# Branch B's scan with the two directions' chunks in one 128x128 product, the backward direction running the sample first

## The chip, the cores and the metric

The kernel runs on one core of one Trainium2 chip. The metric is the device time of one execution in microseconds (us). A core has a matrix engine (TensorE, PE), three others that compute (VectorE DVE, ScalarE ACT, GpSimd POOL) and SyncE (SP), which in this kernel issues every DMA. Each engine works through its own list of instructions in order and waits on semaphores for the others.

## The reference, cut to what matters

A layer runs two branches over 384 tokens (128 of a prompt, 256 of a sample) between one input and one output projection; there are two layers. Branch A is an RWKV-7 mixer. Branch B, which the change touches, is a gated DeltaNet: 8 heads of 128 channels, two directions, chunks of 64 tokens. Prompt and sample are separate sequences: the prompt starts from a zero state, and its final states of both directions are outputs; the sample starts from given states. Per head, direction and chunk:

```
u, wk = t_inv @ (v * beta), t_inv @ (k * beta * exp(gcum))      # t_inv: inverse of I + strictly lower part
v_new = u_i - w_i @ s
o     = (q_i * exp(g_i)) @ s + qk_i @ v_new
s     = s * exp(g_last) + (k_i * exp(g_last - g_i))^T @ v_new
```

The backward direction is the same on reversed tokens. The two outputs are added, normalised, gated and projected. Prompt chunks are 0 and 1, sample chunks 2 to 5; chunks come in three blocks of two, an even chunk on partitions 0 to 63 and an odd one on 64 to 127.

## The kernel before, in words

Large ("dense") products run as float16 passes: three passes of a 128x128 stationary tile against 384 columns for each 128 of the contraction. Their slabs of weights come by 1 MB loads (`st`, line 242), are split into float16 parts by ACT and DVE (`w`, lines 228 and 230), and keep the PE busy for most of the span. The small products of both branches are float32 and are put between the dense passes.

The order on the PE is written out by the program itself: `weave` runs one thread at a time against a modelled clock, which each product advances by columns times a constant. A thread gives way with a modelled wait (`yield HOP`, 1100 ns, one answer of another engine) or until an event of another thread (an inversion: 48000 ns modelled), and when no thread is due, dense passes fill the time. So twelve dense passes usually stand where a thread waits one HOP. The PE's list is then fixed: where the real answer is later than modelled, the PE waits with all that stands behind. The other engines' lists, SP's among them, are made by a scheduler that follows the program's data dependences with the threads' priorities. SP's list holds all loads and stores in one row, so a store that waits for its data holds up the loads behind it.

Branch B has four threads, in order of priority: `gdn_scan`, `gdn_corner`, `gdn_out`, `gdn_front`.

- `gdn_front(h)` prepares a head: the decays `E` (line 1200: DVE writes the exponents' factors, three PE products sum them, ACT takes the exponential), the masked decays `dn` and `dq`, the norms of k and q (`sq` times `ones`, line 1230 on), the token-major `vtok`, `vb` (v times beta, line 1254) and `ktok`, and the scores `Ln` (line 1270) and `QK` (line 1275). After every second head, `invert` runs 30 steps on DVE (lines 542 to 554) for the blocks of 32 of two heads.
- `gdn_corner` makes the 64x64 inverses `Uf` (lines 1291 to 1308) when an inversion is done.
- `gdn_scan(h)` goes through the six chunks of a head in both directions at once, two steps for the prompt and then four for the sample. Both directions are in step 0 of the prompt at chunks 0 and 1, and in step 0 of the sample at 2 and 5. A step has three parts. First, for each direction, the state against KQ (S product, 128x128; none in the prompt's first step); DVE makes `rt` from it (line 1338) and ACT the first part of the output `os`. Second, `Uf` times `rt` or the values, one 64x64 product per direction; ACT makes `vn` (lines 1353, 1355) and `vh` (line 1359) of it. Third, `ktok` times `vh` (64x128, the K product) and `QK` times `vn` (64x64, the Q product) per direction; DVE makes the new state `S` (line 1375) and adds to `os` (line 1381). A HOP stands behind each part.
- The states given for the sample are loaded at the head's start (line 1320) and needed in its third step; the prompt's final states are stored after its second step (line 1388).

The two 64x64 products of a step use opposite corners of the array and run at the same time.

Of the kernel before, what the change touches and what calls it, by code (L numbers as in the profile page):

```python
# [18 lines left out]
T = 384  # L19
NL = 2  # L20
NBLK = 3
# [29 lines left out]
def backbone(ctx: ExitStack, tc: tile.TileContext, i, o):  # L51
# [20 lines left out]
    # Work with many short dependent products is emitted by threads (generators). What a thread yields is the time, by the  # L72
    # cost of the products emitted meanwhile, that its results need before its next products, or the name of an event.
# [17 lines left out]
    def weave(threads, last):  # L91
        """Emits the threads' work; of those that can go on, the first does."""
# [33 lines left out]
    # each half reversed  # L126
# [5 lines left out]
    # sums the four groups of 32 rows  # L132
# [71 lines left out]
    def flag():  # L204
        """The column that takes a low part's sum: neither infinite (overflow) nor tiny everywhere (underflow)."""
        n = n_flag[0]
        n_flag[0] += 1
        return flags[:, n:n + 1]

    def run(fast):  # L210
# [46 lines left out]
        def product(ps, lhs, rhs, nk, ks=None):  # L257
            """ps += sum over k (of ks among nk) of lhs(part, k)^T rhs(part, k), in passes"""
            for kt in ks or range(nk):
                for n, (a, b) in enumerate(passes):  # L260
                    mm(ps, lhs(a, b, kt), rhs(a, b, kt), start=(kt == 0 and n == 0), stop=(kt == nk - 1 and n == len(passes) - 1))
                if kt % STEP == STEP - 1:
                    yield 0

        def finish(g):
            """runs a thread alone; its result"""
            try:
                while True:
                    next(g)
            except StopIteration as e:  # L270
                return e.value

# [4 lines left out]
        def mod_third(l, st, third, take):  # L277
            """One third of the modulation, half by half of its columns; take() gives the tile that they are loaded to."""
# [14 lines left out]
            if third == 2:  # L293
                # the gate's row, with the post-norm's weights, by streams
# [24 lines left out]
        def mod_piece(l, st, k0, k1, take):  # L319
            """Some channel tiles of shift and scale."""  # L320
# [37 lines left out]
        mods, pars = [], []  # L358

        def params(l):  # L360
# [25 lines left out]
            # halves; the rows of the output gates take the scale of their inputs as well  # L386
# [5 lines left out]
            # shift, scale by [channel, third, tile, stream]  # L392
# [4 lines left out]
        def norm_scale(ss):  # L397
            """ss[:, 0] = the norm's scale from two halves' sums of squares"""
# [17 lines left out]
        def layer(l, par, cw, hpar, omka, xs, ready, next_start, after):  # L416
# [5 lines left out]
            def by_channel(ws, n=128):  # L422
                """[channel, token] of a slab"""
# [6 lines left out]
            def by_token(ws):  # L430
                """[token in block, (block, channel)] of a slab"""
# [7 lines left out]
            def dense(tasks):  # L439
                """tasks: (slab, work with its parts); the next slab is loaded and split ahead"""  # L440
# [7 lines left out]
            def gate_tile(n):  # L448
                """tanh of half a channel tile of the merge gates, kept in DRAM"""
# [17 lines left out]
            # [token in block, (dir, head), block]  # L467
            beta, g, neg, vhs, al, ab = (lay.tile([128, 16, 3], F32, tag=t, name=t) for t in ("beta", "g", "neg", "vhs", "al", "ab"))
            # e^{cumulated g}; the same with the two chunks of a block swapped; e^{g left to the chunk's end}; e^{sum} of each chunk
# [18 lines left out]
            def decays():  # L488
# [34 lines left out]
                # neg: -e^g (forward), -beta e^g (backward); vhs: beta ekd (forward), ekd (backward)  # L523
                V.tensor_scalar_mul(neg[:, 0:8], eg[:, 0:8], -1.0)
                V.scalar_tensor_tensor(out=neg[:, 8:16], in0=eg[:, 8:16], scalar=-1.0, in1=beta[:, 8:16], op0=MULT, op1=MULT)
                V.tensor_tensor(out=vhs[:, 0:8], in0=ekd[:, 0:8], in1=beta[:, 0:8], op=MULT)
                V.tensor_copy(vhs[:, 8:16], ekd[:, 8:16])
# [3 lines left out]
            def silu2(ps, bufs=2):  # L531
                """2 silu(x) / cx from x / cx in PSUM"""
# [24 lines left out]
            # ================= branch A: RWKV-7, two heads per channel tile =================  # L557
# [4 lines left out]
            def lora(n):  # L562
                """a slab of the four low-rank inputs, each 96 channels"""
# [34 lines left out]
            def rwkv_tasks(hp):  # L598
                """the pair's projections; what a thread may still read is not overwritten before"""
# [19 lines left out]
            def rwkv_front(hp):  # L619
# [56 lines left out]
                    # [channel, block, slot, 64]; slots of the even chunk then of the odd one:  # L676
                    # AR: r alpha | alpha r, BK: k b | b k; the backward direction has alpha, b and k reversed in time
# [27 lines left out]
                    # masked scores [row slot s, head, parity, block, t]: GA for alpha's columns, GR for r's  # L705
# [53 lines left out]
            def rwkv_corner(hp):  # L759
# [3 lines left out]
                # the inverses of the 64-blocks, negated  # L763
# [22 lines left out]
            def rwkv_back(hp):  # L786
# [6 lines left out]
                # chunk by chunk; y takes the place of a chunk's alpha and r  # L793
# [78 lines left out]
                # bonus, group norm over the head, gate  # L872
# [45 lines left out]
            def proj_tile(dt, heads):  # L918
                """a channel tile of branch A's projection and of the first heads of branch B's, gated, in the place of A's gate"""
# [70 lines left out]
            def out_block(b, d, w):  # L990
                """a block's outputs of a channel tile, gated"""
# [22 lines left out]
            def next_product(n):  # L1014
                """the next layer's first products, four channel tiles at a time"""
# [6 lines left out]
            def last_tiles():  # L1022
                """the last two slabs, block by block; then the residual and the next layer's input"""
# [58 lines left out]
            def spare(n):  # L1082
                """a row tile in the merged parts' place"""
# [6 lines left out]
            def next_input(b):  # L1090
                """the next layer's input: a block's modulated tokens, four channel tiles at a time"""
# [86 lines left out]
            # ================= branch B: gated DeltaNet, one head per channel tile =================  # L1178
# [7 lines left out]

            def gdn_front(h):
# [5 lines left out]
                # [channel, block, slot, 64]: k q | q k  # L1193
# [118 lines left out]
            def gdn_scan(h):  # L1312
# [9 lines left out]
                for stream, order in ((0, [0, 1]), (1, [2, 3, 4, 5])):  # L1322
                    cur = init if stream == 1 else [None, None]
                    for step in range(len(order)):
# [16 lines left out]
                        if cur[0] is not None:  # L1341
                            yield HOP
# [195 lines left out]
```

## Time and profile before

| | |
|---|---|
| median of 3 runs | 3220.7 us (3216.38 to 3223.29) |
| span of the profiled execution | 3223.1 us (the profile gives no time around the span) |
| PE busy | 3009.9 us (93%) |
| DVE busy | 2325.1 us (72%) |
| ACT busy | 1461.4 us (45%) |
| POOL busy | 136.2 us (4%) |
| branch B on the PE, layer 0 | 958.9 to 1457.7 us |
| branch B on the PE, layer 1 | 2535.0 to 3005.5 us |

Busy shares are averages over stages with different limits. The PE's clock has two levels, 2.4 GHz (granted clock 1.0 in the profile) and 1.2 GHz (0.5). A row of the timeline has the start in us, the duration in us, engine, line, operation, output and inputs by the program's names, shapes, and a count when several like ones are put together; in brackets stand the idle time ahead of it and what ended it. A float32 product appears as two passes, so `x4` of a product of the scan is two products. Rows of the PE end later than the next one starts, since passes overlap in the array: costs are read from one start to the next.

### The profile page before, as it was taken

How to read it: one execution, taken by the hardware profiler on the slowest of the kernel's cores; microseconds unless marked ns; L12 is line 12 of the kernel's file. 1: busy time of each engine (PE TensorE's matmuls, PEld its weight loads, DVE VectorE, ACT ScalarE, POOL GpSimd, SP SyncE). 2: the span in 40 equal slices, each digit the busy share in tenths (PEclk: the TensorE clock that was granted, in tenths of full speed). 3: DMA queues.
4: the chain of work that ended last, by engine and by line, in shares of the span. 5: the costliest groups of instructions: out<-in, count | busy, mean ns of one | idle time of the engine just before them, and what ended most of it. 6: DMA issues, size and time to landing. Idle time of an engine off the chain costs nothing. (4 is left out here: it accounts for less than half of the span.)

```text
span 3223.1 us, 70249 instructions
## 1 busy us (share of the span) xinstructions
PE 3009.9 (93%) x28531; PEld 1990.2 (62%) x28531; DVE 2325.1 (72%) x6012; ACT 1461.4 (45%) x3144; POOL 136.2 (4%) x198
## 2 busy tenths in 40 slices
PE   6899999999999999997979999999999999999798
PEld 2466666666665555554976666666666655565388
DVE  3268888888867876765354788887887778887544
ACT  3344444444444555443355444444443446564332
POOL 1000000000000000000000000000000000000000
PEclk8999999999999999998989999999999999999899
DMA  9854444444465335467455545433334442335555
GB/s 342 263 147 132 125 126 133 140 131 139 135 173 159 108 113 159 139 185 201 126 158 156 141 132 149 114 99 91 98 106 123 118 127 71 106 89 167 152 150 160
DMA packets 659018, 457.89 MB, mean 142 GB/s; under 512 B 28858, under 2 KB 627708, under 8 KB 657148
## 3 DMA queue, kind: packets, MB, share of 16 engines
q1 hardware_dynamic: 658684, 453.30, 48.8%
q8 instruction: 227, 3.72, 0.5%
q14 instruction: 107, 0.88, 0.1%
HBM read 421.74 MB, written 31.49 MB: 141 GB/s over the span
## 5 line engine op out<-in xcount | busy, mean ns | idle before, releaser
L78 PE MATMUL jps<-x,w 128*128 128x384 f16 x8640 | 1534.3, 329 | 14.3 <-ACT x L228 7.9
L78 PEld LDWEIGHTS <-w 128*128 128x128 f16 (+1 forms) x10368 | 974.8, 99 | 735.0 <-issue 119.6
L230 DVE SCALAR_TENSOR_TENSOR w<-st,w 128x1024 f16<-128x1024 f32 (+3 forms) x574 | 643.9, 1128 | 239.5 <-ACT w L228 236.5
L228 ACT ACTIVATE w<-st 128x1024 f16<-128x1024 f32 (+3 forms) x574 | 556.3, 978 | 529.4 <-PE jps L78 333.6
L78 PE MATMUL cps<-w,mg 128*128 128x128 f16 x4608 | 265.0, 221 | 11.0 <-ACT mg L228 4.7
L78 PEld LDWEIGHTS <-mg 128*128 128x128 f16 x4608 | 263.6, 99 | 12.7 <-ACT mg L228 5.2
L549 DVE TENSOR_TENSOR ivw<-ivw,ivt 128x30 f32<-128x30 f32 (+4 forms) x720 | 237.6, 330 | 16.4
L547 DVE TENSOR_TENSOR ivt<-ivw 128x30 f32<-128x30 f32 (+4 forms) x720 | 236.8, 329 | 15.7
L78 PE MATMUL jps<-yb,w 128*128 128x384 f16 x744 | 138.9, 337 | 23.1 <-ACT w L228 11.9
L78 PE MATMUL jps<-ya,w 128*128 128x384 f16 x768 | 141.5, 333 | 4.3 <-ACT Uf L1291 1.8
L78 PE MATMUL acc<-wm,cpad 128*32 128x256 f32 (+1 forms) x1664 | 125.6, 384 | 16.0 <-DMA wm<-in_w_mod 15.9
L78 PEld LDWEIGHTS <-x 128*128 128x128 f16 x2304 | 131.3, 98 | 12.7 <-issue 10.0
L78 PE MATMUL jps<-w,x 128*128 128x128 f16 x2304 | 137.1, 220 | 0.0
L867 ACT COPY AR<-cps 64x128 f32<-64x128 f32 x192 | 49.9, 260 | 168.1 <-PE cps L78 163.5
L78 PE MATMUL tps<-AR,BK 64*128 64x128 f32 x768 | 119.0, 288 | 1.3 <-DVE GR L717 1.1
L1340 ACT ACTIVATE os<-cps,gx 64x128 f32<-64x128 f32 x160 | 57.9, 362 | 135.3 <-DVE rt L1338 132.9
L78 PEld LDWEIGHTS tps<-AR,BK 64*128 64x128 f32 x768 | 94.8, 187 | 20.0 <-issue 9.5
L840 DVE COPY Z<-cps 64x128 f32<-64x128 f32 x192 | 55.3, 288 | 60.6 <-PE cps L78 56.8
L730 ACT ACTIVATE nA<-GA 32x192 f32<-32x192 f32 x128 | 46.1, 360 | 108.0 <-DVE GA L715 106.7
L857 DVE SCALAR_TENSOR_TENSOR sring<-cps,pl,sp 64x64 f32<-64x64 f32 x256 | 72.4, 283 | 19.7 <-PE cps L78 15.4
L78 PEld LDWEIGHTS acc<-wm,cpad 128*32 128x32 f32 x1664 | 36.2, 110 | 71.2 <-issue 42.3
L1375 DVE SCALAR_TENSOR_TENSOR S<-S,gx,cps 128x128 f32<-128x128 f32 x128 | 39.1, 343 | 55.7 <-PE cps L78 55.3
(354 smaller groups left out, 3598.8 us busy)
## 6 DMA issues: line engine op xcount, KB each, us to landing
st<-in_w_in SPq DMA_DIRECT2D x194, 1024.0 KB
wm<-in_w_mod SPq DMA_DIRECT2D x176, 512.0 KB
st<-in_w_o SPq DMA_DIRECT2D x32, 1024.0 KB
st<-in_w_pa SPq DMA_DIRECT2D x32, 512.0 KB
gates<-gt SPq DMA_DIRECT2D x64, 192.0 KB
ms<-gates SPq DMA_DIRECT2D x64, 192.0 KB
st<-in_w_pb SPq DMA_DIRECT2D x36, 256.0 KB
wm<-in_w_mod SPq DMA_DIRECT2D x32, 256.0 KB
```

Source lines behind the costliest of these rows:

```text
L78: PE.matmul(out, lhsT=lhsT, rhs=rhs, start=start, stop=stop, **kw)
L228: S.activation(out=dst[0], in_=src, func=AF.Copy, scale=scale)
L230: V.scalar_tensor_tensor(out=dst[1], in0=src, scalar=scale, in1=dst[0], op0=MULT, op1=SUB, accum_out=flag())
L547: V.tensor_tensor(out=tv, in0=W[:, j + 1:32, j:j + 1].to_broadcast([128, n, j]), in1=W[:, j:j + 1, 0:j].to_broadcast([128, n, j]), op=MULT)
L549: V.tensor_tensor(out=W[:, j + 1:32, 0:j], in0=W[:, j + 1:32, 0:j], in1=tv, op=ADD)
L730: S.mul(nA[rq, 6 * d:6 * d + 6, :].rearrange("p (h b) t -> p h b t", h=2), GA[rq, :, p, :, 32 * q:32 * q + 32], -1.0)
L840: V.tensor_copy(dirs[d][4][ar, b, p, :], pb[ar, 0:128])
L857: V.scalar_tensor_tensor(out=sn[hs, hs], in0=pb[hs, o0:o0 + 64], scalar=plc[hs], in1=sp[hs, hs], op0=MULT, op1=ADD)
L867: S.copy(AR[rr, b, 2 * p:2 * p + 2, :].rearrange("p a b -> p (a b)"), pas[d][rr, 0:128])
L1340: S.activation(out=os_[d][R_, b, :], in_=pas[d][R_, 0:128], func=AF.Copy, scale=egs[R_, x, b:b + 1])
L1375: V.scalar_tensor_tensor(out=new[d], in0=cur[d], scalar=glast[:, p, x, b:b + 1], in1=pas[d][:, 128:256], op0=MULT, op1=ADD)
```

## The change

- One step now handles forward chunk s and backward chunk 5-s, s from 0 to 5. Forward runs prompt then sample, backward sample then prompt. At each step the two chunks lie in different halves of the partitions, so both are rows of one 128-row tile.
- `Uf` and `QK` are tiles of six 128x128 matrices, one per step, with the forward chunk's 64x64 block and the backward chunk's on one diagonal (other zero blocks are cleared once per layer by eight POOL memsets). Four tiles of each are kept, for heads modulo 4. A step has one U product and one Q product of 128x128 in place of two each of 64x64. The K products take all 128 rows of `ktok`, with zeros in `vh` for the other direction's rows (scales `vh0`, `vh1`), so `vn` is one ACT instruction and `vh` one per direction.
- Beta of the backward direction moves into `Uf`'s columns (DVE instead of ACT); `vb` is gone; `rt` is copied from `vtok` where a direction starts without a state.
- The tile `dn` is gone: `E` itself, a single buffer, is masked in place and read by `Ln` and by half of `QK`. `QK` is written by four DVE instructions of 64x192 instead of one of 128x384. The sums of q's norm are three products of 128 columns instead of six of 64.
- The backward state of the sample is needed in step 0; the forward one in step 2. The forward prompt state is stored at step 2, the backward prompt state after step 5. Every step has three HOPs; before, the prompt's first step had two.

The core of the diff (deleted comments and blank lines left out):

```diff
+            u_ring, qk_ring = ([Q.tile([128, 6, 128], F32, tag=f"{n}{q}", name=f"{n}{q}") for q in range(4)] for n in ("Uf", "QK"))
+            for t in (*u_ring, *qk_ring):
+                G.memset(t, 0.0)
+            def by_step(t, d, p, c0, n):
+                r = slice(64 * p, 64 * p + 64)
+                return t[r, p::2, c0:c0 + n] if d == 0 else t[r, 1 - p::2, c0:c0 + n][:, ::-1]
...
                 E = Q.tile([128, 9, 64], F32, tag="E", name="E", bufs=1)
...
-                dn = Q.tile([128, 2, 3, 64], F32, tag="dn", name="dn", bufs=1)
+                V.tensor_tensor(out=E[:, 0:6, :], in0=E[:, 0:6, :], in1=half["lt"].unsqueeze(1).to_broadcast([128, 6, 64]), op=MULT)
...
-                for c in range(6):
-                    b, p = divmod(c, 2)
-                    mm(t[64 - 64 * p:128 - 64 * p, b:b + 1], sq[:, 64 * c:64 * c + 64], ones[:, 0:1])
+                for b in range(NBLK):
+                    mm(t[:, b:b + 1], sq[:, 128 * b:128 * b + 128], ones[:, 0:1])
...
-                vb = Q.tile([128, NBLK, 128], F32, tag="vb", name="vb", bufs=4)
-                V.tensor_tensor(out=vb, in0=vt, in1=bc(beta[:, 8 + h, :], 128), op=MULT)
...
-                V.tensor_tensor(out=QK, in0=tv[:, :, 64:128].unsqueeze(1).to_broadcast([128, 2, NBLK, 64]), in1=dq, op=MULT)
+                for d in range(2):
+                    for p in range(2):
+                        r = slice(64 * p, 64 * p + 64)
+                        V.tensor_tensor(out=by_step(QK, d, p, 64 - 64 * p, 64), in0=tv[r, :, 64:128], in1=(E[r, 6:9, :] if d else dq[r]), op=MULT)
...
-                for stream, order in ((0, [0, 1]), (1, [2, 3, 4, 5])):
-                    cur = init if stream == 1 else [None, None]
...
-                            mm(pb[A_, 0:128], Uf[A_, d, b, :], vals[d])
...
-                                mm(pas[d][:, 128:256], kt_[A_, b, :], vhs_[d][A_])
...
-                            mm(pb[R_, 128:256], QK[A_, d, b, :], vns[d][A_])
+                cur = [None, init[1]]
+                for s in range(6):
+                    if s == 2:
+                        nc.sync.dma_start(out=o["new_state_delta"][0, l, 0, h], in_=cur[0])
+                        cur[0] = init[0]
+                    elif s == 4:
+                        cur[1] = None
+                    for d, c in enumerate((s, 5 - s)):
...
+                            mm(pas[d][:, 0:128], KQ[:, b, 2 * p:2 * p + 2, :], cur[d])
...
+                    yield HOP
+                    pb = cps()
+                    mm(pb[:, 0:128], Uf[:, s, :], rt)
+                    vn = Q.tile([128, 128], F32, tag="vn", name="vn", bufs=1)
+                    S.mul(vn, pb[:, 0:128], vns[:, h, s:s + 1])
+                    going = [d for d in range(2) if s != (5, 3)[d]]
+                    for d in going:
+                        vhs_[d] = Q.tile([128, 128], F32, tag="vh", name="vh", bufs=2)
+                        S.mul(vhs_[d], pb[:, 0:128], (vh0, vh1)[d][:, h, s:s + 1])
+                    yield HOP_V * HOP
+                    for d in going:
+                        mm(pas[d][:, 128:256], kt_[:, at[d][0], :], vhs_[d])
+                    mm(pb[:, 128:256], QK[:, s, :], vn)
...
+                    yield HOP
+                nc.sync.dma_start(out=o["new_state_delta"][0, l, 1, h], in_=cur[1])
```

Three places of the engines' lists show what the change moves. The first is PE's list of a scan step of the first head in layer 0 (`jps` is a dense pass, `rt,Uf` the U product, `vh,ktok` K, `vn,QK` Q), before and then after:

```order
9727 L78 MATMUL cps<-rt,Uf 64x128 x2
9728 L85 MATMUL tps<-ident,p_11779 128x128 x3
9729 L78 MATMUL tps<-KQ 64x128 x6
9730 L78 MATMUL cps<-vh,ktok 128x128 x2
9731 L78 MATMUL cps<-vn,QK 64x128 x2
9732 L78 LDWEIGHTS w_11940
9733 L78 MATMUL jps<-x_198,w_11940 128x384
```

```order
9727 L78 MATMUL cps<-rt,Uf_11096 128x128
9728 L85 MATMUL tps<-ident,p_11789 128x128 x3
9729 L78 MATMUL tps<-KQ 64x128 x6
9730 L78 MATMUL cps<-vh,ktok 128x128 x2
9731 L78 MATMUL cps<-vn,QK_11100 128x128
9732 L78 LDWEIGHTS w_11950
9733 L78 MATMUL jps<-x_198,w_11950 128x384
```

The U and Q pairs have become one product each, and what stands around them is in its place.

The second is SP's list where head 0's scan ends and head 1's begins in layer 0 (`S<-in_state_delta` loads a given state, `out_new_state_delta<-S` stores a prompt state), before and then after:

```order
270 L1388 DMA out_new_state_delta<-S 128x128 x2
271 L285 DMA wm<-in_w_mod 128x1024
272 L242 DMA st<-in_w_in 128x16x128
273 L285 DMA wm<-in_w_mod 128x1024
274 L1320 DMA S<-in_state_delta 128x128 x2
275 L456 DMA gates<-gt 128x384
276 L242 DMA st<-in_w_in 128x16x128
```

```order
273 L285 DMA wm<-in_w_mod 128x1024
274 L456 DMA gates<-gt 128x384
275 L242 DMA st<-in_w_in 128x16x128
276 L1347 DMA S<-in_state_delta 128x128
277 L1403 DMA out_new_state_delta<-S 128x128
278 L1347 DMA S<-in_state_delta 128x128
279 L285 DMA wm<-in_w_mod 128x1024
```

The load of the forward state, the store of the previous head's backward state and the load of the backward state now stand in this order; the pair of loads has been parted by the store.

The third is DVE's list around the end of head 1's front in layer 0, where the next head's `E` is written; before and then after:

```order
1409 L1200 TENSOR_TENSOR E<-b_le,g 128x192
1410 L1200 TENSOR_TENSOR E<-b_lt,g 128x192
1411 L1226 TENSOR_SCALAR rs<-tps 128x3
1412 L1200 TENSOR_TENSOR E<-b_ge,g 128x192
1413 L1238 TENSOR_SCALAR rs<-tps 128x3
...
1423 L1270 TENSOR_TENSOR Ln<-tps,dn 128x384
1424 L1275 TENSOR_TENSOR QK<-tps,dq 128x384
1425 L1274 SCALAR_TENSOR_TENSOR nB<-Ln,m_122,nB 128x192
1426 L542 STREAM_TRANSPOSE ivw<-nB 128x1024
```

```order
1421 L1287 TENSOR_TENSOR Ln<-tps,E 128x384
1422 L1295 TENSOR_TENSOR QK_11101<-tps,dq 64x3x64 x2
1423 L1291 SCALAR_TENSOR_TENSOR nB<-Ln,m_122,nB 128x192
1424 L1295 TENSOR_TENSOR QK_11101<-tps,E 64x3x64 x2
1425 L551 STREAM_TRANSPOSE ivw<-nB 128x1024
1426 L1219 TENSOR_TENSOR E<-b_le,g 128x192
1427 L556 TENSOR_TENSOR ivt<-ivw 128x30
1428 L1219 TENSOR_TENSOR E<-b_lt,g 128x192
1429 L558 TENSOR_TENSOR ivw<-ivw,ivt 128x30
1430 L1219 TENSOR_TENSOR E<-b_ge,g 128x192
```

The `E` of head 2 stood ten rows and more ahead of head 1's `Ln`; now it stands behind `Ln`, the four parts of `QK`, `nB` and the inversion's first transpose.

## Rows read from the trace of the kernel before

**Rows 1.** Windows, branch B by layer: us, busy (count) by engine, PEclk, DMA, GB/s.

```profile
958.90:1457.70 498.80, 477.40 (x3716) 284.84 (x3716) 370.45 (x979) 257.10 (x629) 18.27 (x19) 0.98 0.50 144
2535.00:3005.50 470.50, 442.90 (x3313) 271.98 (x3311) 357.84 (x961) 249.96 (x620) 19.21 (x19) 0.96 0.38 109
```

**Rows 2.** Waits of PE: for whom, us in all, times, longest.

```profile
PE tps L85 <- DVE os L1398: 9.5, 2, 4.7
PE tps L78 <- DVE iva L554: 8.6, 3, 4.3
PE cps L78 <- ACT vh L1359: 6.1, 15, 1.1
```

**Rows 3.** Timeline of PE through one scan step: start us, us, what.

```profile
1048.36 0.61 PE L78 MATMUL cps<-S,KQ 128*128 128x128 f32 x4
1048.81 0.83 PE L78 MATMUL tps<-ones,sq 128*128 128x1 f32 x6
1049.50 1.14 PE L78 MATMUL jps<-x,w 128*128 128x384 f16 x6
1050.57 0.43 PE L78 MATMUL cps<-rt,Uf 64*64 64x128 f32 x4
1050.93 0.52 PE L78 MATMUL tps<-ones,sq 128*64 128x1 f32 x12
1051.38 2.12 PE L78 MATMUL jps<-x,w 128*128 128x384 f16 x12
1053.43 0.49 PE L78 MATMUL cps<-vh,ktok 64*128 64x128 f32 x4
1053.86 0.44 PE L78 MATMUL cps<-vn,QK 64*64 64x128 f32 x4
1054.22 1.15 PE L78 MATMUL jps<-x,w 128*128 128x384 f16 x6
1055.21 0.83 PE L78 MATMUL tps<-ident,rs 128*128 128x128 f32 x6
```

**Rows 4.** Timeline of PE, DVE and SP around a state's store.

```profile
1096.90 0.49 PE L78 MATMUL cps<-vh,ktok 64*128 64x128 f32 x4
1097.43 0.60 DVE L1375 SCALAR_TENSOR_TENSOR S<-S,gx,cps 128x128 f32<-128x128 f32 x2
1097.80 1.64 SPq L1388 DMA_DIRECT2D out_new_state_delta<-S  x2
```

**Rows 5.** Timeline of SP and DVE: two loads of 192 KB and their readers.

```profile
1367.77 0.34 SPq L925 DMA_DIRECT2D ga<-gates  x1
1371.12 0.56 DVE L928 SCALAR_TENSOR_TENSOR ga<-ga,jps 128x384 f32<-128x384 f32 x1 [2.00 <-DMA ga<-gates]
1376.84 0.34 SPq L925 DMA_DIRECT2D ga<-gates  x1
1381.77 0.56 DVE L928 SCALAR_TENSOR_TENSOR ga<-ga,jps 128x384 f32<-128x384 f32 x1 [2.25 <-DMA ga<-gates]
```

**Rows 6.** Timeline of DVE and PE at head 1's scores.

```profile
988.36 0.56 DVE L1270 TENSOR_TENSOR Ln<-tps,dn 128x384 f32<-128x384 f32 x1
989.44 0.42 DVE L1274 SCALAR_TENSOR_TENSOR nB<-Ln,m,nB 128x192 f32<-128x192 f32 x1
989.89 1.95 DVE L542 STREAM_TRANSPOSE ivw<-nB 128x1024 f32<-128x1024 f32 x1
994.75 0.35 DVE L1215 TENSOR_TENSOR dq<-E,b_le 128x192 f32<-128x192 f32 x1
991.18 0.49 PE L78 MATMUL tps<-E,m_gt 128*128 128x192 f32 x2
```

**Rows 7.** Windows: an inversion, and a stretch behind it.

```profile
1061.90:1115.00 53.10, 46.34 (x315) 26.90 (x313) 48.82 (x136) 27.72 (x70) 1.07 (x2) 0.97 0.42 122
1115.70:1119.10 3.40, 3.40 (x44) 1.70 (x44) 1.21 (x5) 2.06 (x6) 0.00 (x0) 0.50 0.14 33
```

**Rows 8.** Timeline of POOL at branch B's start, layer 0.

```profile
965.22 1.36 POOL L1239 TENSOR_TENSOR rs<-rs,mhalf 128x6 f32<-128x6 f32 x1 [8.70 <-DVE rs L1238]
```

More of the change, by code (lines that the diff above doesn't have):

```diff
@@ L464, in gate_tasks @@
                 return [(*gate_tile(gate_n[0] - n + q), steps) for q in range(n)]
-            beta, g, neg, vhs, al, ab = (lay.tile([128, 16, 3], F32, tag=t, name=t) for t in ("beta", "g", "neg", "vhs", "al", "ab"))
+            beta, g, neg, al, ab = (lay.tile([128, 16, 3], F32, tag=t, name=t) for t in ("beta", "g", "neg", "al", "ab"))
+            vns, vh0, vh1 = (lay.tile([128, 8, 6], F32, tag=t, name=t) for t in ("vns", "vh0", "vh1"))
             gx = lay.tile([128, 5, 16, 3], F32, tag="gx", name="gx")
@@ L1268, in gdn_front @@
                 Ln = Q.tile([128, 2, NBLK, 64], F32, tag="Ln", name="Ln", bufs=2)
-                QK = Q.tile([128, 2, NBLK, 64], F32, tag="QK", name="QK", bufs=4)
-                V.tensor_tensor(out=Ln, in0=tv[:, :, 0:64].unsqueeze(1).to_broadcast([128, 2, NBLK, 64]), in1=dn, op=MULT)
+                QK = qk_ring[h % 4]
+                V.tensor_tensor(out=Ln, in0=tv[:, :, 0:64].unsqueeze(1).to_broadcast([128, 2, NBLK, 64]), in1=E[:, 0:6, :].rearrange("p (d b) t -> p d b t", d=2), op=MULT)
                 lv = Ln.rearrange("p d b t -> p (d b) t")
@@ L1274, in gdn_front @@
                 V.scalar_tensor_tensor(out=nv, in0=lv[:, :, 32:64], scalar=m01[:, 3:4], in1=nv, op0=MULT, op1=ADD)
-                V.tensor_tensor(out=QK, in0=tv[:, :, 64:128].unsqueeze(1).to_broadcast([128, 2, NBLK, 64]), in1=dq, op=MULT)
-                act["front", h] = KQ, kt_, vt, vb, QK, rs[:, 3:6], Ln
+                for d in range(2):
+                    for p in range(2):
+                        r = slice(64 * p, 64 * p + 64)
+                        V.tensor_tensor(out=by_step(QK, d, p, 64 - 64 * p, 64), in0=tv[r, :, 64:128], in1=(E[r, 6:9, :] if d else dq[r]), op=MULT)
+                act["front", h] = KQ, kt_, vt, QK, rs[:, 3:6], Ln
                 event(("front", l, 8 + h), 0)
@@ L1285, in gdn_corner @@
                 for hh in range(2):
-                    Ln = act["front", h0 + hh][6]
+                    Ln = act["front", h0 + hh][5]
                     i0 = 6 * hh
-                    Uf = Q.tile([128, 2, NBLK, 64], F32, tag="Uf", name="Uf", bufs=4)
+                    Uf = u_ring[(h0 + hh) % 4]
                     for q in range(2):
                         for d, a in ((0, a1), (1, a2)):
-                            S.mul(Uf[:, d, :, 32 * q:32 * q + 32], a[:, i0 + 3 * d:i0 + 3 * d + 3, :], m01[:, q:q + 1])
-                    xc = Q.tile([128, 6, 32], F32, tag="xc", name="xc", bufs=2)
+                            for p in range(2):
+                                r = slice(64 * p, 64 * p + 64)
+                                dst, src = by_step(Uf, d, p, 64 * p + 32 * q, 32), a[r, i0 + 3 * d:i0 + 3 * d + 3, :]
+                                if d == 0:
+                                    S.mul(dst, src, m01[r, q:q + 1])
+                                else:
+                                    V.scalar_tensor_tensor(out=dst, in0=src, scalar=m01[r, q:q + 1], in1=bc(beta[r, 8 + h0 + hh, :], 32), op0=MULT, op1=MULT)
+                    xc = Q.tile([128, 6, 32], F32, tag="xc", name="xc", bufs=1)
                     qs = [(slice(64 * p, 64 * p + 32), slice(64 * p + 32, 64 * p + 64)) for p in range(2)]
@@ new lines, in gdn_scan @@
+                cur = [None, init[1]]
[5 more added lines that the diff above has]
+                        cur[1] = None
+                    pas, at = [cps(), cps()], []
+                    for d, c in enumerate((s, 5 - s)):
+                        b, p = divmod(c, 2)
+                        at.append((b, p, 8 * d + h, slice(64 * p, 64 * p + 64), slice(64 - 64 * p, 128 - 64 * p)))
+                        if cur[d] is not None:
+                            mm(pas[d][:, 0:128], KQ[:, b, 2 * p:2 * p + 2, :], cur[d])
+                    rt = Q.tile([128, 128], F32, tag="rt", name="rt", bufs=1)
+                    for d in range(2):
+                        b, p, x, A_, R_ = at[d]
+                        val = vt[A_, b, :]
+                        if cur[d] is not None:
+                            V.scalar_tensor_tensor(out=rt[A_], in0=pas[d][A_, 0:128], scalar=neg[A_, x, b:b + 1], in1=val, op0=MULT, op1=ADD)
+                            S.activation(out=os_[d][R_, b, :], in_=pas[d][R_, 0:128], func=AF.Copy, scale=egs[R_, x, b:b + 1])
+                        else:
+                            V.tensor_copy(rt[A_], val)
+                    yield HOP
[4 more added lines that the diff above has]
+                    going = [d for d in range(2) if s != (5, 3)[d]]
+                    vhs_ = {}
+                    for d in going:
+                        vhs_[d] = Q.tile([128, 128], F32, tag="vh", name="vh", bufs=2)
+                        S.mul(vhs_[d], pb[:, 0:128], (vh0, vh1)[d][:, h, s:s + 1])
+                    yield HOP_V * HOP
+                    new = [None, None]
+                    for d in going:
+                        mm(pas[d][:, 128:256], kt_[:, at[d][0], :], vhs_[d])
+                    mm(pb[:, 128:256], QK[:, s, :], vn)
+                    for d in going:
+                        b, p, x, A_, R_ = at[d]
+                        new[d] = Q.tile([128, 128], F32, tag="S", name="S", bufs=6)
+                        if cur[d] is not None:
+                            V.scalar_tensor_tensor(out=new[d], in0=cur[d], scalar=glast[:, p, x, b:b + 1], in1=pas[d][:, 128:256], op0=MULT, op1=ADD)
+                        else:
+                            S.copy(new[d], pas[d][:, 128:256])
+                    for d in range(2):
+                        b, p, x, A_, R_ = at[d]
+                        if cur[d] is not None:
+                            V.tensor_tensor(out=os_[d][R_, b, :], in0=os_[d][R_, b, :], in1=pb[R_, 128:256], op=ADD)
+                        else:
+                            S.copy(os_[d][R_, b, :], pb[R_, 128:256])
+                    cur = new
+                    yield HOP
```

92 lines of the change are left out of this document (17 added, 75 removed).

## The prediction

> **What bounds the kernel now.** I read the page's table of busy time first, and cut branch B's two stretches out of it by windows: there the PE is busy 477.4 of 498.8 us and 442.9 of 470.5 us, DVE 74 and 76% [rows 1]. So the PE's list is what takes the time, and only 21 and 28 us of it are gaps. The table of waits puts names on the larger ones: the end of the last head's scan, 4.7 us once a layer, and the end of an inversion, up to 4.3 us [rows 2]. Inside an inversion the second limit shows: DVE is busy 48.8 of 53.1 us [rows 7]. The rest was read in the timeline of a scan step, and then in the order of the changed lists, for what the PE will wait for there.
>
> **The products.** Costs go from one start to the next [rows 3]. Six dense passes take 0.99 us (1054.22 to 1055.21, a 128x128 product behind them), 0.165 each. Six of them ahead of the U pair take 1.07 (1049.50 to 1050.57): entering another shape of array costs 0.08 to 0.09. U's four passes take 0.36 until the next start. Two 128x128 products take 0.45 (1048.36 to 1048.81, four passes), so one is 0.22. U before is 0.09 + 0.36 = 0.45, after 0.22: 0.23 less, six times a head, 1.4 us.
> K and Q before: 0.09 + 0.43 (1053.43 to 1053.86) + 0.36 (to 1054.22) = 0.88 in five steps and 0.45 in the last, which has only Q: 4.85 a head. After: two K and one Q in four steps (0.66), one and one in two (0.44): 3.5. That is 1.35 less. The q norm's twelve passes of 128x64 take 0.45 (1050.93 to 1051.38), six of 128x128 0.69 (1048.81 to 1049.50): with an entry where it stood alone, about 0.15 more. Per head 1.4 + 1.35 - 0.15 = 2.6 us, for 16 heads 42. Where a small product stands beside another one (the scores `KQ`, 128x64, stay as they are) a change of shape remains. Going through both lists product by product with these prices gives 2924 against 2886 us for the PE's whole list. I take -38.
>
> The Trainium skill, TensorEngine Tiling (Array Packing), section Key Properties, says that changing the tiling mode drains the engine; the 0.08 to 0.09 at a change of shape agrees. The same page (Theoretical Speedup) says that contractions of 64 rows gain up to twofold by sharing the array, which speaks against filling half the stationary tile with zeros; that is the third rival below.
>
> **A new wait: the backward state behind a store.** Before, both loads of a head's given states stand together on SP, and no product needs them until the third step. Now the backward state is needed in the first product of step 0, and its load stands behind the store of the previous head's last state, which waits for DVE's `S` of that head's last step. This holds for the heads that follow directly on another: five in layer 0, six in layer 1; the others have a gap or other work between. From the K product's start the store's issue follows after 0.90 us (1096.90 to 1097.80), and two issues take 1.64 [rows 4]; so the load is issued some 1.4 us after K. Its landing no row shows. Loads of 192 KB were used 3.35 us (1367.77 to 1371.12) and 4.93 us (1376.84 to 1381.77) after their issue, both awaited [rows 5]. Those two are of one size and differ by 1.6, so what else is in the rings counts as much as bytes. For 64 KB the bounds are a third of the first, 1.1, and the first itself, 3.35; I take 2.7. State ready at 1.4 + 2.7 = 4.1 us after K. The PE gets there after K and Q (0.44) and twelve dense passes (1.96), 2.4 us, at seven heads; at four, where a half filled hop stands there, at about 1.75. Stall 7 x 1.7 + 4 x 2.35 = 21 us; with the bounds 4 and 28.
> Behind the store on SP stand `wm` and `st` loads too. They come up to 2 us later than now; the slabs are loaded one ahead and I cost this at nothing, because the previous slab's products still run meanwhile; were that cover gone, the PE would wait for `w`, by no more than these 2 us at a head.
>
> **A second one: E behind QK.** `E` has one buffer and is now read by `Ln` and by half of `QK`; so the next head's `E` stands behind these. At head 1 it stands behind the inversion's transpose as well. From the rows: `Ln` starts at 988.36, next 0.47 later; four parts of `QK` at no more than 0.35 each (the 128x192 mask at 994.75 has as many columns), some 1.2; `nB` 0.42 and the transpose 1.95 bring it to 992.4; three `E` with two of the inversion's operations between, 1.2, end at 993.6. The PE wants the first at 991.18 [rows 6]. It waits about 2.5 us, at head 2 of both layers. By the same count along the lists it waits about 2 at head 3 of layer 0, and 0.3 to 0.7 at heads 1, 3 (layer 1) and 7: 8 us, bounds 4 and 12.
>
> **The other engines.** DVE gets 166 instructions more (`QK` in four, backward `Uf`, `rt` copies; `vb` gone), about 2 us a head at 0.2 to 0.35 each. It is covered by the PE except inside inversions, which end about a microsecond later for 8 times: +5, of which some falls in the modelled 48 us; I take +3. On ACT the four instructions behind a U pair (two `vn`, two `vh`) become three, or two; the PE waited 6.1 us for `vh` in all [rows 2], of which I take -2. The eight memsets come before POOL's first power, in front of which POOL is idle for 8.7 us [rows 8]: nothing, as long as they take under 1 us each. The last steps of a layer have nothing dense beside them; with a HOP more in each head's first step about twelve passes fewer are left there: +3 for both layers. Where a stall falls into an inversion in which the PE would have waited at its end anyway (8.6 us in all, and 4.3 the longest [rows 2]), it costs nothing: -5.
>
> **The clock.** Behind the wait for an inversion the granted clock was 0.50 for 3.4 us, 1.2 GHz [rows 7]; 44 passes done then would have taken half, so such a drop costs 1.7 us. I expect it behind two of the new stalls, not behind all: +3.
>
> **Sum.** -38 + 21 + 8 + 3 - 2 + 3 - 5 + 3 = -7 on the span of 3223.1 us, 3216. No time around the span is shown; the span lies 2.4 us above the median of 3220.7, within its runs. Against the median the sum would be 3214; between the two I forecast 3215, no difference that can be told: a measurement of this kernel tells about 0.2%, 6.4 us.
>
> **Rivals.**
> - The gain stays. If the loads land in 1.1 to 1.6 us and `E` costs 4, the sum is -38 + 5 + 4 + 3 - 2 + 3 - 5 = -30, 3191. For it: the load is a third of those in [rows 5], and the store ahead of it is small. Against it: the store's own wait, which no landing takes away.
> - Slower by the stalls and the clock. Place: step 0 of the eleven heads. If the state takes as long as 192 KB do (3.35 us, stalls 28 us), every stall is about 2.4 us or more and each is followed by 3.4 us at 1.2 GHz, 1.7 us: 11 x 1.7 = 19. The sum is -38 + 28 + 10 + 3 - 2 + 3 - 5 + 19 = +18, 3239. It decides from a landing of about 3 us. For it: the clock fell behind an inversion's wait; against it: most of the waits in between are shorter.
> - The pair was already sharing the array. A pair of 64x64 products needs 0.36 us with the way out, 0.27 without, against 0.22 for one full product; if the rest were not saved (no drain of its own, only a lag that the next product has anyway), U and Q save 0.05 each and K nothing: 16 x (12 x 0.05) = 10 less, q's norm 2 more; -8 + 21 + 8 and the small terms' +2 make +23, 3244. The Trainium skill's rule of packing (above) is this reading. Against it: the six passes at 0.99 and at 1.07 and the late start behind U stand in one step [rows 3].
> - Nothing is bound by these products: DVE's inversion sets the phase. Then the PE's saving inside the inversions (four windows of 40 to 54 us a layer) is waited away at their ends. The list fills the modelled 48 us with dense passes, however, so this takes only a few us, within the forecast's own range.
>
> **How the numbers follow.** Forecast 0.42, its own range 3204 to 3228; gain stays 0.26; stalls and clock 0.24; packing 0.05; the rest 0.03. Faster by over 0.2%: 0.26 and a third of the forecast's 0.42, 0.40. Slower: 0.24 + 0.05, 0.29. Same: 0.31. The range takes in most of the two neighbours: 3190 to 3240.
>
> **What would show it.** Right: the product of U at 0.22 us between its neighbours without 0.09 ahead of it; a PE wait at the first `S` product of a head that ends with a DMA of `S`, 1 to 3 us at up to eleven heads, 20 us in all; a PE wait for `E` of 2 to 3 us at head 2 of both layers; windows of branch B shorter by 3 to 8 us in all. Wrong: the first `S` product without a wait (then the time is nearer 3191), or stretches of clock 0.50 behind most heads' starts (then 3239), or U and Q with gaps on both sides as before.

## The result, and the profile after

The changed kernel took 3262.8 us (3253.8 to 3263.5, 4 runs) against 3222.0 us of the kernel before; the ratio is 1.0125, with a 95% interval of 1.0104 to 1.0146. It is slower by 40 us, outside the predicted range of 3190 to 3240 us, and the forecast was 7 us faster. A second measurement beside later experiments gave 1.0119 [1.0102, 1.0136].

A profile shows a single execution, and executions of one kernel differ here by up to some 10 us, so a profile's total can lie that far from the median to which the ratio belongs. The profiled execution of the changed kernel (3253.8 us, span 3251.8) was the quickest of its four, and it is 28.7 us longer than the one before. All of that is in branch B; outside its stretches the execution is 3 us shorter. Windows of its two stretches, with the columns of [rows 1]:

```profile
957.70:1477.10 519.40, 467.06 (x3480) 308.15 (x3478) 393.84 (x1067) 240.43 (x571) 26.16 (x28) 0.96 0.49 138
2547.20:3039.30 492.10, 430.40 (x3073) 291.93 (x3071) 380.00 (x1048) 232.07 (x562) 21.73 (x26) 0.94 0.38 104
```

These end at the last transposition of `os`, 5 us behind those of [rows 1]; the windows of before up to the same place:

```profile
958.90:1462.90 504.00, 477.85 (x3719) 284.90 (x3717) 372.79 (x987) 258.08 (x635) 19.12 (x20) 0.98 0.49 142
2535.00:3010.60 475.60, 443.26 (x3314) 272.00 (x3312) 360.19 (x969) 250.95 (x626) 20.06 (x20) 0.95 0.38 108
```

So the stretches are 31.9 us longer; PE is busy 23.7 us less (921.1 to 897.5), and its gaps grew by 55.5 us, from 58.5 to 114.0. DVE is busy 773.8 us instead of 733.0.

The products did what was expected. A step in PE's timeline, beside [rows 3]:

```profile
1057.85 1.14 PE L78 MATMUL jps<-x,w 128*128 128x384 f16 x6
1058.82 0.38 PE L78 MATMUL cps<-rt,Uf 128*128 128x128 f32 x2
1059.05 0.73 PE L78 MATMUL tps<-ones,sq 128*128 128x1 f32 x6
1061.58 0.61 PE L78 MATMUL cps<-vh,ktok 128*128 128x128 f32 x4
1062.03 0.39 PE L78 MATMUL cps<-vn,QK 128*128 128x128 f32 x2
1062.25 1.14 PE L78 MATMUL jps<-x,w 128*128 128x384 f16 x6
```

Six dense passes ahead of U take 0.97 us, so nothing is paid for a change of shape; U takes 0.23 us, two K products 0.45, Q 0.22. The table of PE's waits over the whole execution shows which waits took the gain (compare [rows 2]):

```profile
PE cps L78 <- DMA S<-in_state_delta: 18.8, 11, 3.9
PE jps L78 <- DVE w L230: 16.7, 10, 4.6
PE cps L78 <- DVE rt L1368: 7.3, 12, 1.0
PE cps L78 <- ACT os L1369: 7.3, 10, 1.0
PE tps L85 <- ACT th L1144: 6.4, 1, 6.4
PE tps L78 <- DVE E L1219: 5.2, 2, 2.9
```

Of these, the kernel before had no wait for the state or for DVE's `E`; its line for the splits on DVE was:

```profile
PE jps L78 <- DVE w L230: 8.9, 15, 3.2
```

Now branch B alone in both traces, with the waits added up by what ended them. Waits for the state's loads took 18.9 us, none before. Splits of weights (`w`) took 12.6, 1.3 before. The scan's answers (`rt`, `os` of the same step, `vn`, `vh`, `S`) took 24, 11 before. DVE's `E` took 8.7, of which 3.5 stands under an operation of the inversion (`ivt`) that ended later; none before. The convolution (`p`, `th`) took 13, 5 before. Waits for norms (`sq`, `rs`, `ss`) fell from 15 to 9.

The state, in the timeline of SP and PE between heads 0 and 1 of layer 0 (compare [rows 4]):

```profile
1086.92 0.38 SPq L242 DMA_DIRECT2D st<-in_w_in  x1
1087.35 1.70 SPq L1347 DMA_DIRECT2D S<-in_state_delta  x1
1091.69 0.34 SPq L1403 DMA_DIRECT2D out_new_state_delta<-S  x1
1092.08 0.43 SPq L1347 DMA_DIRECT2D S<-in_state_delta  x1
1094.08 0.46 PE L78 MATMUL cps<-S,KQ 128*128 128x128 f32 x2 [1.48 <-DMA S<-in_state_delta]
```

The order is that of the lists: slab, forward state, store, backward state, and 2.0 us after the last issue PE goes on. `E` at head 2, on DVE and PE (compare [rows 6]):

```profile
989.85 1.91 DVE L551 STREAM_TRANSPOSE ivw<-nB 128x1024 f32<-128x1024 f32 x1
991.69 0.31 DVE L1219 TENSOR_TENSOR E<-b_le,g 128x192 f32<-128x192 f32 x1
992.15 0.56 PE L78 MATMUL tps<-E,m_gt 128*128 128x192 f32 x2 [1.74 <-DVE ivt L556]
```

The term that I had priced at a few us shows behind the end of an inversion. DVE and PE behind the third one of layer 0 (rows of the scan's `S`, `os` and `ss` on DVE are left out):

```profile
1233.64 2.00 DVE L563 STREAM_TRANSPOSE iva<-ivw 128x1024 f32<-128x1024 f32 x1
1236.35 0.31 DVE L1317 SCALAR_TENSOR_TENSOR Uf<-iva,m,beta 64x96 f32<-64x96 f32 x1
1237.16 1.64 DVE L1317 SCALAR_TENSOR_TENSOR Uf<-iva,m,beta 64x96 f32<-64x96 f32 x5
1238.91 0.31 DVE L1317 SCALAR_TENSOR_TENSOR Uf<-iva,m,beta 64x96 f32<-64x96 f32 x1
1239.32 0.32 DVE L1317 SCALAR_TENSOR_TENSOR Uf<-iva,m,beta 64x96 f32<-64x96 f32 x1
1239.74 0.95 DVE L230 SCALAR_TENSOR_TENSOR w<-st,w 128x768 f16<-128x768 f32 x1
1240.76 2.58 PE L78 MATMUL jps<-ya,w 128*128 128x384 f16 x8 [4.11 <-DVE w L230]
```

The same place before the change has the split 0.6 us behind the inversion:

```profile
1223.38 1.99 DVE L554 STREAM_TRANSPOSE iva<-ivw 128x1024 f32<-128x1024 f32 x1
1225.42 0.55 DVE L928 SCALAR_TENSOR_TENSOR ga<-ga,jps 128x384 f32<-128x384 f32 x1
1225.97 1.22 DVE L230 SCALAR_TENSOR_TENSOR w<-st,w 128x1024 f16<-128x1024 f32 x1
1225.42 0.85 PE L78 MATMUL tps<-iva,Ln 32*32 32x32 f32 x24 [2.78 <-DVE ss L1395]
```

Eight `Uf` operations of 0.31 us, with the rank of the corner's thread, now come between, about 2.6 of the 4.1 us; the rest is the scan's `S` and `os`. The slab waits for them, and PE waits 4.1 us for the slab. Not all of this is new: PE had waited 2.8 us here before, to the inversion's end. At the two other large waits of this kind in branch B (3.9 us from 1377 on, 4.6 us at 2948) the waits for `w` had been 0.4 and 0.9 us, with 1.8 for `Uf` at the second.

### The profile page after: what moved, and what is told of

Same layout as the page of the kernel before. It is cut to its first block, busy times and chain, and to the rows that moved or that the text cites. A ratio compares the mean times of both kernels' runs of the same rounds, so it can differ in the third digit from the quotient of the medians.

```text
span 3251.8 us, 69400 instructions
## 1 busy us (share of the span) xinstructions
PE 2985.1 (92%) x28051; PEld 2029.9 (62%) x28051; DVE 2366.9 (73%) x6178; ACT 1424.4 (44%) x3016; POOL 151.6 (5%) x220
## 5 line engine op out<-in xcount | busy, mean ns | idle before, releaser
L78 PEld LDWEIGHTS <-w 128*128 128x128 f16 (+1 forms) x10368 | 991.2, 100 | 732.4 <-issue 112.3
L78 PE MATMUL acc<-wm,cpad 128*32 128x256 f32 (+1 forms) x1664 | 127.6, 386 | 15.6 <-DMA wm<-in_w_mod 15.5
L78 PEld LDWEIGHTS <-x 128*128 128x128 f16 x2304 | 131.5, 98 | 12.6 <-issue 10.0
L1006 DVE TENSOR_TENSOR og<-cps,gp 128x128 f32<-128x128 f32 x96 | 27.7, 288 | 69.8 <-ACT junk L1005 69.8
```

What stands on the lines that cost most here:

```text
L78: PE.matmul(out, lhsT=lhsT, rhs=rhs, start=start, stop=stop, **kw)
```

## The experiments

The experiments were to tell two readings apart. Theory W: the new waits of PE cost what they last, and add up. Rival D: DVE's list is behind in and after the inversions and sets the pace; a wait that goes comes back as another. Stretches of half clock belong to both.

**The store on another queue.** Edit of the changed kernel:

```diff
-                nc.sync.dma_start(out=o["new_state_delta"][0, l, 1, h], in_=cur[1])
+                nc.gpsimd.dma_start(out=o["new_state_delta"][0, l, 1, h], in_=cur[1])
```

> The changed kernel with one edit: the store of the backward prompt state is issued by POOL instead of SP, so both loads of a head's given states stand together on SP again; PE's list is the same. Theory W (the new waits add up one by one): the 18.8 us that PE waited for the loaded state go, and with them some of the stretches at half clock: 18 to 24 us faster than the changed kernel, about 3240 us. Rival D (DVE's list is behind in the inversions, and sets the pace there; a wait that goes comes back as another): no more than 10 us faster, about 3253.

Ratio 1.0104 [1.0087, 1.0121], 7 us less than with 1.0125, a difference that lies within the two intervals. It was no good test of W, since most of the wait stayed (8 us of it went, with these 7 us of time); SP and PE where head 1 begins:

```profile
1089.75 0.38 SPq L242 DMA_DIRECT2D st<-in_w_in  x1
1090.18 2.16 SPq L1347 DMA_DIRECT2D S<-in_state_delta  x2
1095.94 0.46 PE L78 MATMUL cps<-S,KQ 128*128 128x128 f32 x2 [0.50 <-DMA S<-in_state_delta]
```

and in the table of PE's waits:

```profile
PE cps L78 <- DMA S<-in_state_delta: 10.8, 7, 2.9
```

Without the store the pair is still issued at the head's start, behind a 1 MB slab, and lands too late at seven heads. The store had added some 8 us to that.

**The order alone.** The kernel before with the six steps of the changed one (`for d, c in enumerate((s, 5 - s))`, `cur = [None, init[1]]`, three HOPs a step); 64x64 products, `vb`, `dn` and `QK` stay.

> The kernel before with the order alone (backward runs the sample first, six steps with three HOPs); products of 64x64, beta, E and QK as before. Theory W: PE waits for the loaded state at eleven heads, 19 us, a few us for the longer first steps, and no product is saved: 18 to 25 us slower than before, about 3243. Rival D: 5 to 12 us slower.

Ratio 1.0109 [1.0092, 1.0126]: 35 us, more than both. Its windows:

```profile
960.40:1483.50 523.10, 489.73 (x3718) 291.42 (x3717) 375.03 (x987) 259.81 (x635) 21.14 (x20) 0.97 0.48 137
2557.40:3050.60 493.20, 452.77 (x3314) 276.95 (x3312) 361.63 (x968) 252.53 (x626) 19.44 (x20) 0.94 0.37 104
```

Waits for the state are 14.6 us, where the kernel before had none. PE is also busy 21 us longer (942.5 against 921.1); a later experiment tells these apart.

**E in place alone.** The kernel before with `E` masked in place and read by `Ln` and half of `QK` (no `dn`).

> The kernel before with the decays masked in place in E (no dn, QK in two instructions): the next head's E stands behind Ln and QK. Theory W: PE waits for E some 8 us: 5 to 12 us slower than before, about 3230. Rival D: within 4 us of before, since DVE issues only 16 instructions more.

Ratio 1.0019 [1.0004, 1.0035], 6 us; PE waits 9.1 us for DVE's `E` where it waited for none. The median is in W's range, but the interval, 1 to 11 us, takes in much of D's as well.

**Beta in Uf alone.** The kernel before, with

```diff
-                            S.mul(Uf[:, d, :, 32 * q:32 * q + 32], a[:, i0 + 3 * d:i0 + 3 * d + 3, :], m01[:, q:q + 1])
+                            for p in range(2):
+                                r = slice(64 * p, 64 * p + 64)
+                                dst, src = Uf[r, d, :, 32 * q:32 * q + 32], a[r, i0 + 3 * d:i0 + 3 * d + 3, :]
+                                if d == 0:
+                                    S.mul(dst, src, m01[r, q:q + 1])
+                                else:
+                                    V.scalar_tensor_tensor(out=dst, in0=src, scalar=m01[r, q:q + 1], in1=bc(beta[r, 8 + h0 + hh, :], 32), op0=MULT, op1=MULT)
```

and without `vb`.

> The kernel before with beta of the backward direction in Uf's columns, by DVE in the shapes of the changed kernel (no vb). DVE gets eight instructions of 0.31 us for a pair of heads right behind an inversion. Theory W: within 4 us of before. Rival D: they hold up the splits of the weights behind an inversion, where PE then waits: 8 to 15 us slower than before, about 3233.

Ratio 1.0069 [1.0052, 1.0087]: 22 us, more than either expected. To see whether the burst on DVE does it, the same with the eight instructions on POOL:

```diff
+                                    G.tensor_tensor(out=dst, in0=src, in1=bc(bm[r, q, h0 + hh, :], 32), op=MULT)
```

> The kernel before with beta in Uf's columns as in b3, but the eight instructions of a pair on POOL. If b3's 22 us come from the burst on DVE behind an inversion, the ratio is 0.999 to 1.002; if they come from elsewhere (the smaller shapes on ACT, vb gone), it stays at 1.005 to 1.008.

Ratio 1.0006 [0.9995, 1.0017]. 20 of the 22 us are gone, with `vb` still gone and ACT's shapes still small: it is the burst. Windows of the two, DVE first:

```profile
954.90:1467.60 512.70, 481.16 (x3719) 285.86 (x3717) 382.79 (x1027) 256.56 (x619) 18.45 (x20) 0.97 0.49 140
2540.30:3030.10 489.80, 451.00 (x3312) 275.79 (x3311) 369.56 (x1008) 249.75 (x610) 20.21 (x20) 0.93 0.37 105
```

```profile
955.20:1463.80 508.60, 479.70 (x3720) 285.63 (x3718) 373.79 (x995) 256.89 (x619) 32.16 (x52) 0.97 0.48 141
2534.30:3009.10 474.80, 441.82 (x3312) 271.51 (x3311) 360.54 (x976) 249.72 (x610) 38.03 (x52) 0.95 0.37 108
```

18 us of DVE work (752.4 to 734.3) moved to POOL are worth 19 us of the stretches. How the burst costs this is not quite as D had it. Against the kernel before, the stretches with the burst on DVE are 23 us longer, half of it gaps of PE (70.3 us against 58.5) and half its busy time (932.2 against 921.1), at a lower granted clock (0.97 and 0.93 against 0.98 and 0.95). And the gaps are not for the slabs alone: waits for `p` rose by 5 us, for `ga` by 3.5 and for `w` by 3. On POOL those for `p` (10.3 to 4.3) and `ga` (4.4 to none), which DVE makes, went again; those for `w` did not (4.5 to 6.8).

**The state loaded ahead.** The changed kernel with

```diff
+                    s0 = Q.tile([128, 128], F32, tag="S0", name="S0", bufs=2)
+                    nc.sync.dma_start(out=s0, in_=i["state_delta"][0, l, 1, hn])
...
+                    elif s == 3 and h < 7:
+                        load(h + 1)
```

> The changed kernel with the backward state of the next head loaded in the fourth step of the head before, to two tiles of its own (the table of flags is cut from 1024 to 768 columns for the space, which saves a transpose or two at the very end). PE waits for no state any more. Theory W: the 18.8 us of the changed kernel go: ratio to before 1.006 to 1.007 in place of 1.0125. Rival D (DVE sets the pace in the inversions): 5 to 10 us go, ratio 1.009 to 1.011.

Ratio 1.0059 [1.0042, 1.0075], in W's range: no wait for the state is left, and 21 us are gone for 18.9 us of waiting. The profile agrees less well. Its execution took 3251.0 us (the median is 3243.3), and other waits have grown in it: for `p` and `th` 17.0 us in branch B in place of 13.0, for the inversion 12.0 in place of 7.4, for the scan's answers 27 in place of 24. The line with the longest:

```profile
PE tps L85 <- DVE p L1263: 11.5, 4, 10.0
```

In the changed kernel the product that waits these 10.0 us had waited 6.4, for `th`. So here, too, some waits took another's place, as D has it, and that the whole gain is the state's wait is shown by the times alone.

**Uf on POOL in the changed kernel.**

> The changed kernel with the backward half of Uf (eight instructions for a pair of heads) made by POOL instead of DVE, with beta and the mask multiplied once per layer. If the burst on DVE right behind an inversion is what costs (22 us in the kernel before with beta in Uf), 10 to 20 us go: ratio 1.006 to 1.009; the waits for w (12.6 us) shrink to a few. If it is DVE's load as a whole, 2.5 us less DVE work per pair is worth 0 to 6 us: ratio 1.0105 to 1.0125.

Ratio 1.0104 [1.0087, 1.0121], about 7 us less, at the edge of the second reading's range, though the waits for `w` fell from 10.0 us (DVE's part) to 1.9, as in the first. With the state still late (18.5 us) the profile has a new wait, behind the very inversion shown above:

```profile
PE tps L78 <- DVE yv L1428: 5.5, 1, 5.5
```

The granted clock in layer 1 is 0.93 against 0.94, which says little, as this profiled execution (3261.2 us) lies 4 us above its median and that of the changed kernel 9 us below. Here a wait did take another's place, as D has it. So in the changed kernel the burst, taken out alone, is worth about 7 us and not the 20 that it was worth in the kernel before.

**Three repairs together.** As the last two, and `yield (4 if h in (2, 3, 6) else 2) * HOP` behind `E`.

> The changed kernel with three repairs: the backward state loaded ahead, the backward half of Uf on POOL, and the PE products of E two HOPs later at heads 2, 3 and 6. If the costs add up, 19 + 12 + 9 us go and some clock: level with before, ratio 0.998 to 1.002. If they replace one another, ratio 1.004 to 1.008.

Ratio 0.9975 [0.9963, 0.9988]: 8 us faster than before, 48 faster than the changed kernel, a little more than the first reading had. One by one two of the repairs gave 21 and 7 us, and `E` cost 6 in the kernel before (its repair was not run alone, nor any pair); together they give more than the sum, 34. Why is open: waits for DVE's `E` fell from 8.7 to 4.0 us only, and the third repair also shifts PE's list, and a shift of the list can be worth 10 us by itself (y5 below). Its windows:

```profile
959.50:1454.70 495.20, 459.16 (x3479) 304.79 (x3477) 381.77 (x1035) 238.68 (x571) 43.77 (x60) 0.98 0.51 145
2530.80:3008.30 477.50, 427.22 (x3073) 293.24 (x3071) 368.69 (x1016) 231.80 (x562) 38.81 (x58) 0.95 0.38 108
```

At the granted clock of before, 0.98 and 0.95, PE is busy 886.4 us against 921.1: the products save 35 us, close to the predicted 38.

**The order, with the state loaded ahead.**

> The kernel before with the order alone, as in b1, and the backward state of the next head loaded ahead. In b1 the order cost 35 us; its profile shows 15 us in waits for the state, and PE busy 21 us more, about 6 of that by the clock: 15 us of PE's own work, from single K products and a first step with a HOP of its own. If that reading is right the wait goes and the work stays: ratio 1.004 to 1.007. If the whole 35 us came from the late state, the ratio is 0.999 to 1.002.

Ratio 1.0066 [1.0043, 1.0088]. The wait goes (14 us from b1) and 21 us stay. PE is busy 15.5 us more than before:

```profile
955.20:1469.70 514.50, 484.44 (x3719) 290.67 (x3718) 374.25 (x987) 259.13 (x635) 21.36 (x20) 0.97 0.49 139
2541.80:3030.40 488.60, 452.18 (x3313) 277.56 (x3311) 360.13 (x968) 252.08 (x626) 19.24 (x20) 0.93 0.37 105
```

So with 64x64 products the order itself costs PE work: two steps a head have a single K product, which shares the array with none. The trace shows a pair of K products and a single one, each with the Q pair behind it:

```profile
1050.33 0.49 PE L78 MATMUL cps<-vh,ktok 64*128 64x128 f32 x4
1050.75 0.43 PE L78 MATMUL cps<-vn,QK 64*64 64x128 f32 x4
1064.01 0.48 PE L78 MATMUL cps<-vh,ktok 64*128 64x128 f32 x2
1064.42 0.44 PE L78 MATMUL cps<-vn,QK 64*64 64x128 f32 x4
```

From start to start the pair takes 0.42 us and the single product 0.41. Two singles in place of a pair are thus 0.4 us more a head, by estimate 7 us for 16 heads. Most of the rest of the 15.5 goes with the lower granted clock (0.97 and 0.93 against 0.98 and 0.95). With 128 rows a single K product takes half of the two that took 0.45 above, so this extra is not paid there.

**A longer HOP.** As y3, with `yield HOP_V * HOP` behind the S product.

> The changed kernel with the three repairs (as y3) and a HOP longer by a fifth behind the S product, as the kernel already has behind the U product. In y3 PE still waits 11.6 us for rt and os there. If these waits are answers that come just late, half of them go: ratio 0.994 to 0.997 in place of 0.9975. If DVE's queue sets them, they move along: 0.997 to 1.000.

Ratio 0.9944 [0.9926, 0.9962], 18 us faster than before: the first reading's figure, but by luck, since the waits it named stayed (11.1 us for `rt` and `os`, 11.6 in y3). The gain over y3 is 10 us by the ratios. In the profiles it is in layer 1, 460.0 us in place of 477.5, with 2.6 us more in layer 0; the two differ by more than 10 because y3's profiled execution (3223.6 us) was 7 us above its median. Which of the shifted instructions does it is open.

```profile
959.10:1456.90 497.80, 460.91 (x3480) 306.55 (x3478) 383.76 (x1035) 239.11 (x571) 40.60 (x60) 0.97 0.51 144
2531.80:2991.80 460.00, 420.25 (x3072) 290.47 (x3071) 368.17 (x1016) 231.69 (x562) 40.69 (x58) 0.96 0.40 112
```

**The changed kernel again.**

> The changed kernel itself on the chip of these runs, to compare with: ratio to before 1.0125 as measured, within 0.002.

Ratio 1.0119 [1.0102, 1.0136], as expected.

## Why the prediction was wrong

- **The products** (-38): right. PE's busy time fell by 35 us where the clock is equal (y3), and by 23.7 in the changed kernel, whose clock is lower in both layers.
- **The state behind the store** (+21): the size was right, 18.9 us at eleven places, and 21 us of time when it was taken out (y1). The cause was half seen, so the size owes something to luck: x1 shows that the late issue of the pair, behind a slab, makes 10.8 us of the wait with or without the store.
- **E behind QK** (+8): right, 8.7 us of waits, and about 6 us of time alone (b2, interval 1 to 11).
- **The other engines** (+3 for DVE, -2 for ACT): this step failed. It said of DVE's added work that "it is covered by the PE except inside inversions, which end about a microsecond later for 8 times", and took +3. The amount was nearly right (DVE is busy some 2.5 us more a head, 2 were expected), but the inversions did not get longer: from the first transpose to the last, all eight take 380 us in place of 378. The work is not spread over a head: eight of the instructions stand right behind the end of an inversion, in front of what has queued up there for DVE. Put there alone they cost 22 us, and 20 of these go when POOL does them (b3, b4); in the changed kernel waits for `w` rose by 11 us, and taking the eight off DVE alone gave back 7 us (y2). I had counted instructions and not looked at what stands behind them. That the slabs behind the store came later, which the prediction took at nothing, is not the reason: with the store on POOL the waits for `w` on DVE stay (x1: 9.7 us, against 10.0), with `Uf` on POOL they go (y2: 1.9).
- **The scan's answers**, -2 in the same step: PE's waits for `rt`, `os`, `vn`, `vh` and `S` rose by 13 us instead, the largest miss of a single term. Why is not shown; y5's longer HOP did not lower those for `rt` and `os`.
- **The clock** (+3): mis-sized. Dense passes at 1.2 GHz, counted by start-to-start times near 0.33 us in the two stretches, rose from 63 to 116; at 0.163 us lost on each that is 9 us.
- **What is absorbed** (-5): the waits for norms fell by 6 us, those for the inversion stayed at about 8. The +3 for the last steps of a layer was not measured by itself; its waits are among the scan's answers.

With the measured sizes the sum is -32 (products, without the clock) + 19 + 9 + 11 (`w`) + 13 (scan) + 8 (`p`, `th`) - 6 (norms) + 9 (clock) = +31, of 32 in the stretches of the two profiles. It is an account of one execution each; that its parts can be taken out one by one is not shown, and y1 to y3 show that they cannot quite.

The rival that named the stalls and the clock (3239) had the right sign, by the wrong mechanism: it wanted 28 us of stalls and 19 of clock, and 19 and 9 were seen. Neither the packing rival nor the one in which the gain stays was seen. That DVE's inversion sets the phase, which I set aside as "only a few us", came nearest to what DVE did: not through the inversion's length, which stayed, but through what queues behind it.

## What to carry to other kernels

Where an engine's backlog ends, an instruction put in front of the queue delays what waited (here 18 us of DVE work cost 19 us of the stretches, b3 and b4); price an added instruction by its place in the list, not by its engine's mean share. A load that is moved from late use to first use has to be issued a phase earlier. A change whose core is right can lose by its fittings: with the state or `Uf` repaired alone the kernel stayed slower than before, and with all three repairs it was 8 us faster.

## What was not expected of the hardware

- A single product of 64 rows takes as long as a pair that shares the array: 0.41 us from start to start against 0.42 (b5, 1064.01 and 1050.33, both behind dense passes).
- The 64 KB state was used 1.6 us after the end of its issue behind a store (1092.51 to 1094.08); behind a 1 MB slab issued 2 us earlier it took 3.6 us (x1: 1092.34 to 1095.94). Counted from the start of the issue, as in the prediction, both are 0.4 us more, 2.0 and 4.0; my bounds of 1.1 and 3.35 us left out the upper one.
- The eight 64x96 operations of a pair of heads took 0.31 us each on DVE and cost 22 us in all behind the inversions (b3); on POOL they took 0.35 us in the median and cost nothing that shows (ratio 1.0006, b4).
